# One tile and one cadence for the modulation sums of a hybrid mLSTM and gated-delta block, from the first solve pairs to the last output product

## The chip, the cores and the metric

The kernel runs on one core of a Trainium2 chip. A core has a matrix engine (TensorE, "PE" in the profile, with its weight loads as "PEld"), a vector engine (VectorE, "DVE"), a scalar engine (ScalarE, "ACT"), GpSimd ("POOL"), and a queue engine SyncE ("SP") that issues most of the loads. Sixteen DMA engines carry the transfers of all queues. Each engine works through its own stream of instructions in order; semaphores order the streams among each other.

The metric is the device time in microseconds (us) of one execution. The program was run three times before the change, and the median counts.

## What is computed

One layer of a bidirectional block on 256 tokens of 2048 channels. Cut to what matters here:

```python
mod = c_act @ ada_w + ada_b          # c_act = silu(c): one row of 2048; ada_w: 2048 x 12288
shift_m, scale_m, gate_m, shift_f, scale_f, gate_f = jnp.split(mod[:, None, :], 6, axis=-1)
h = rms_norm(x, norm_mix_w) * (1 + scale_m) + shift_m
proj = h @ w_in                       # q, k, v, gates of both branches, merge gates
y_a = (sigmoid(a_o) * rms(mlstm_bidir(...))) @ w_branch_a
y_b = (rms(gated_delta_bidir(...)) * silu(b_z)) @ w_branch_b
x = x + gate_m * ((g_a * y_a + g_b * y_b) @ w_out)
hf = rms_norm(x, norm_ffn_w) * (1 + scale_f) + shift_f
gt, up = jnp.split(hf @ w_gate_up, 2, axis=-1)
x = x + gate_f * ((silu(gt) * up) @ w_down)
out = rms_norm(x, norm_final_w)
```

The gated delta branch has 16 heads; each needs the inverse of unit lower triangular 64 x 64 matrices, made here by block inversion.

## The kernel before

**Products.** Every weight matrix is used once. A job loads it in pieces of 1 MB through SP into the tile `raw` (three buffers). ACT rounds each half of a piece to the high part `wh`, DVE subtracts to get the low part `wl` (three buffers each), and TensorE multiplies high by high, high by low and low by high. `fjob` makes 128 output channels from one piece; `tjob` makes 512 output channels from four pieces (weights 512 wide, 12 products to a half). After the products of each half stands a call of `pump()`. So the whole kernel has a count of halves, and that count is used in this document: half n is the one whose products stand just before the n-th call of `pump()`. It was counted by going through the loops by hand.

**The modulation sums.** Parts 0 and 1 of `mod` are made in the first stage. Parts 2 (`gate_m`), 3 (`shift_f`) and 4 (`scale_f`) are made later, 16 columns of 128 values each, so 48 sums. One sum is a load of 1 MB (tile `ada`, issued on SP by `ask()`, L116) and one DVE instruction that multiplies 128 x 2048 values with the broadcast row and adds them up (`add()`, L124). Part 5 (`gate_f`, 16 sums) follows in the FFN with a cadence of eight halves. Where `ask` and `add` go is decided in `pump()` and `sums()`:

- `every[0]`: a sum is owed at each call whose count is a multiple of it; 0 means none is owed and none is asked for.
- `held[0]`: true in the first three of the nine steps of a solve pair; while it is true nothing is added.
- `age[0]`: calls of `pump()` since the last `ask()`. A sum is added only if that is over two.
- `room[0]`: the pool, the tag, the number of buffers and the number of transfers that may be outstanding. At first it is one tile (`rows_p`, tag `ada`). From the a-branch's output product on it is a pool `sr` with three tiles, and then `sums()` keeps three transfers asked for ahead of each sum.

Instructions wrapped in `order(...)` are kept behind the instruction that stands before them on their engine; others may be moved ahead of them by the scheduler, which lays out each engine's stream when the program is built. `ask` and `add` are wrapped; the loads and splits of a `tjob` are not.

**The stages around the change.**

1. Four groups g = 0 to 3 of four heads. Before each group a triangular inversion (`gdn_invert`): DVE makes 32 x 32 inverses, POOL stores them (L696) and loads them back in another layout into `cg` (L723), DVE transposes `cg` (L725) and mixes it to `R` (L729, L730), ACT copies parts to `X` (L738). The first solve product (L761, `p<-R,cc`) needs `R`. Meanwhile TensorE works on product jobs (`fill`).
2. In each group two pairs of heads go through `gdn_phase2` (nine steps), between them the `fjob`s of the next heads (`b_job`) and their `gdn_phase1`. In groups 0 to 2 the pairs span halves 63 to 94, 118 to 149 and 173 to 204; in group 3 halves 228 to 253.
3. The first two mLSTM heads and the rest of the merge gates, to half 258; the b-branch's output product `y_b` (halves 259 to 290) beside the mLSTM heads; the a-branch's output product `y_a` (291 to 322); there `gate_m` is spread over the partitions (`row_diag`, `row_spread`, at halves 292, 296, 300, 304) and the merged branches are transposed (`merged`).
4. The last output product `o_job` 0 to 3 (halves 323 to 350 and the last piece of job 3, which goes by tokens). Before its end all of parts 3 and 4 must be there: `sums(P)` makes what is left, and `affn` is made of part 4. Then RMSNorm, and the FFN.

**Where the sums stand before the change**, by this count: the adds of group 0 at halves 67, 71, 75, 84, 88, 92, those of groups 1 and 2 at the same distances from their start (122, 126, 130, 139, 143, 147 and 177, 181, 185, 194, 198, 202), those of group 3 at 232, 236, 240, 245, 249, 253. Each `ask` follows one half after the add before it; the seventh, 13th and 19th are asked for at halves 93, 148 and 203, at the end of a group, and wait through the inversion. After the pairs there are none until half 270; then adds at 273, 277, 281, 285 and 289, one more at the end of `y_b`, three transfers asked for at once at the start of `y_a`, adds at 291, 292 and every fourth half to 320, and nine in the output product at 327, 330, 333, 336, 341, 344, 347, 349 and 351.

Of the kernel before, what the change touches and what calls it, by code (L numbers as in the profile page):

```python
# [9 lines left out]
F32 = mybir.dt.float32  # L10
# [5 lines left out]
P = 128  # L16
T = 256
D = 2048
# [34 lines left out]
def hybrid_block(ctx: ExitStack, tc: tile.TileContext, xr, nfr, crow, pk_d, cst_d, ada2, ada4, win0, winb, wint, wba, wbb, wo, wgu, wd, out, dbg=None):  # L53
# [3 lines left out]
    def pool(stack, name, bufs=1, **kw):  # L57
        return stack.enter_context(tc.tile_pool(name=name, bufs=bufs, **kw))
# [3 lines left out]
    rows_p = pool(ctx, "rows")  # L62
# [9 lines left out]
    def order(ins, yes=True):  # L72

        return tc.keep_in_program_order(ins) if yes else ins
# [30 lines left out]
        order(S.activation(row_c[:, g * 512 : (g + 1) * 512], pc_, AF.Silu))  # L105


    room = [(rows_p, "ada", 1, 1)]
    asked, unasked, age = [], [], [0]

    def ask():

        pl, tag, bufs, _ = room[0]
        part, b = unasked.pop(0)
        raw = pl.tile([P, D], F32, tag=tag, bufs=bufs, name=f"ada{part}_{b}")
        order(nc.sync.dma_start(raw, ada4[part - 2, b]))  # L116
        asked.append((part, b, raw))
        age[0] = 0

    def add():  # L120

        part, b, raw = asked.pop(0)
        c = part * KB + b
        order(V.scalar_tensor_tensor(raw, raw, 1.0, row_c[:, :D], ALU.mult, ALU.mult, accum_out=mod[:, c : c + 1]))  # L124
        if b == KB - 1:
            c = slice(part * KB, part * KB + KB)
            V.tensor_tensor(mod[:, c], mod[:, c], pk[:, PK_ADAB + c.start : PK_ADAB + c.stop], ALU.add)
# [11 lines left out]
    def settle(keep=0, only=None):  # L139

        now = [f for f in behind if only is None or f.__name__ == only]
        for f in now[: len(now) - keep]:
            behind.remove(f)
            f()

    count, every = [0], [0]
    owed, held = [0], [False]

    def sums(n=1):

        while n and (unasked or asked):
            while unasked and len(asked) < room[0][3]:
                ask()
            add()
            n -= 1

    def pump():
        count[0] += 1
        age[0] += 1
        if every[0] and count[0] % every[0] == 0:  # L160
            owed[0] = 1
        if room[0][3] > 1:
            if owed[0]:
                owed[0] = 0
                sums()
        elif asked:
            if owed[0] and age[0] > 2 and not held[0]:
                owed[0] = 0
                add()
        elif unasked and every[0]:  # L170
            ask()

    def fjob(name, src, done):
# [95 lines left out]
    def fill(n=1):  # L269

        while n and fills:
            if next(fills[0], None):
                n -= 1
            else:
                fills.pop(0)
# [90 lines left out]
    def z_job(g, early=0):  # L366
        def done(ps):
            szs[g] = evp.tile([P, 2, 512], F32, tag="sz", bufs=1, name=f"sz{g}")
            for t in range(2):
                S.activation(szs[g][:, t], ps[t], AF.Silu)  # L370
        return tjob(f"z{g}", [wint[g, u] for u in range(4)], hh, hl, done, early)
# [121 lines left out]
    with ExitStack() as s0:  # L493
# [18 lines left out]
        def loads(b):  # L512
            ra = [w0.tile([P, D + 2], F32, tag="ra", bufs=5, name=f"ra{b}_{i}") for i in range(2)]
            raw = st.tile([P, N0, P], F32, tag="raw", bufs=3, name=f"raw0_{b}")
            for i in range(2):
                order(nc.sync.dma_start(ra[i], ada2[b, :, i]))
            order(nc.sync.dma_start(raw, win0[b]))
            return ra, raw
# [10 lines left out]
        ra, raw = loads(0)  # L529
# [18 lines left out]
        for b in range(KB):  # L548
            if b:
                ra, raw = loads(b)  # L550
# [137 lines left out]
    def gdn_invert(g):  # L688

        uu = uus.pop(g)  # L690
        tmp = bk.tile([64, 256], F32, tag="utmp", bufs=1, name=f"utmp{g}")
        inv = inv_d[g].rearrange("j b (x h) i -> h (b x) j i", h=GRP)

        def store(rows):
            for e in range(GRP):
                G.dma_start(inv[e, :, rows], uu[16 * e : 16 * e + 16, rows])  # L696

        yield
        order(V.memset(uu.rearrange("p j i -> p (j i)")[:, ::33], 1.0))
        size = 0  # L700
        for i in range(30, 0, -1):
            w = 31 - i
            t3 = tmp[:, 0 : i * w].rearrange("p (j c) -> p j c", j=i)
            order(V.tensor_tensor(
                t3,
                uu[:, 0:i, i : i + 1].broadcast_to([64, i, w]),
                uu[:, i : i + 1, i + 1 :].broadcast_to([64, i, w]),
                ALU.mult,
            ))
            order(V.tensor_tensor(uu[:, 0:i, i + 1 :], uu[:, 0:i, i + 1 :], t3, ALU.add))  # L710
            if i == 16:
                store(slice(16, 32))
            size += i * w + 125
            if size > 720:
                size = 0
                yield
        store(slice(0, 16))
# [300 lines left out]
    def invert(g):  # L1018
        gen = gdn_invert(g)
        next(gen)  # L1020
        fill(4 if g else 6)
        for _ in gen:
            fill(1)

    invert(0)
    for g in range(4):
        blocks = gdn_blocks(g)
        next(blocks)
        fill(8)
        next(blocks)  # L1030
        fill(1)
        pairs = [gdn_phase2(g, p) for p in range(2)]
        if g == 3:
            settle()
            sf.close()
            mq["pool"] = pool(sq_, "mq", side="right")
            first2 = [mlstm(h) for h in range(2)]
            for c in first2:
                next(c)
        every[0] = 1  # L1040
        for p in range(2):
            pieces = stream(4 * g + 2 * p + 4)
            for n in range(1, 10):

                held[0] = n < 4
                if p == 0:
                    next(blocks, None)
                next(pairs[p], None)
                if g == 3 and n == (8, 4)[p]:
                    next(first2[p])  # L1050
                for _ in range(last[n] if g == 3 else second[n] if p else after[n]):
                    next(pieces)
            for _ in pairs[p]:
                pass

            if g < 3:
                while 4 * g + 2 * p + 5 not in heads:
                    next(pieces)
        if g < 3:
            fills.insert(0, z_job(g + 1))  # L1060
            every[0] = owed[0] = 0
            invert(g + 1)
    settle()
    sx.close()
# [53 lines left out]
            yield from y_b(g)  # L1118

    o4s = [o_load(g) for g in range(2)]  # L1120
    every[0] = owed[0] = 0
    cores = steps(*first2)
    fill(1)
    next(cores)
# [19 lines left out]
    o_split(3, o4s[3])  # L1144
    fill(2)
    drive(cores, 3)
    every[0] = 1
    drive(steps(mlstm(2), mlstm(3)), 3)
    fill(1000)
    mgh, mgl = big(bigC, F32R, "mgh"), big(bigC, F32R, "mgl")  # L1150
    sm_.close()
    sr_ = ExitStack()
    if asked:
        add()
    room[0] = (pool(sr_, "sr"), "sr", 3, 3)
    gm = room[0][0].tile([P, D], F32, name="gm")
    dgs = {}

    def row_diag(part, g, rp):
        ms = mods[:, part == 5]  # L1160
        if not g:
            m = mod[:, part * KB : (part + 1) * KB]
            V.tensor_copy(ms[:, 0], m)
            V.tensor_tensor(ms[:, 1], m, ms[:, 0].bitcast(F32), ALU.subtract)
        dg = dgs[part, g] = rp.tile([P, 2, 4, P], F32R, tag="dg", bufs=2, name=f"dg{part}_{g}")
        for i in range(2):
            V.tensor_tensor(
                dg[:, i], ident.unsqueeze(1).broadcast_to([P, 4, P]),
                ms[:, i, 4 * g : 4 * g + 4].bitcast(F32).unsqueeze(2).broadcast_to([P, 4, P]), ALU.mult,
            )  # L1170
# [6 lines left out]
            PE.matmul(pr, onesr, woven(dg[:, i]), start=i == 0, stop=i == 1)  # L1177
        S.activation(woven(dst[:, g * 512 : (g + 1) * 512]), pr.rearrange("p (c h) -> p c h", h=2), AF.Copy)

    every[0] = 4  # L1180
    for g in range(4):
        for i, _ in enumerate(y_a(g)):
            if g and i == 3:
                merged(g - 1, mgh, mgl)
            if i in (1, 5) and g < 2:
                row_diag(2, 2 * g + i // 4, room[0][0])
            if i in (3, 7) and g < 2:
                row_spread(2, 2 * g + i // 4, gm)
    every[0] = 0


    def o_job(g, front=None):
# [112 lines left out]
    for g in range(4):  # L1305
        if g == 3:
            root()
        for i, _ in enumerate(o_job(g, front_o if g == 3 else None) if g else o_first, 0 if g else 2):
            if i in ((4, 7), (2, 5), (2, 5), (0, 2))[g]:
                sums()  # L1310
            if g == 3 and i == 4:
                sums(P)
                V.scalar_tensor_tensor(
                    affn, mod[:, 4 * KB : 5 * KB], 1.0, pk[:, PK_NFFN : PK_NFFN + KB], ALU.add, ALU.mult
                )
    if dbg is not None and "x1" in dbg:
        G.dma_start(dbg["x1"], x1)
    room[0] = (rows_p, "ada", 1, 1)
    ada_parts(5)
    sw.close()  # L1320
    sr_.close()
# [73 lines left out]
    for j in range(FB // 4):  # L1395
# [4 lines left out]
        for e2 in range(2):  # L1400
            px = gps(f"pxf{j}_{e2}")
            for e in range(2):
                f = 2 * e2 + e
                for t in range(2):
                    PE.transpose(px[:, e * T + t * P : e * T + (t + 1) * P], sg[:, t, f * P : (f + 1) * P], ident)
            b = 4 * j + 2 * e2
# [156 lines left out]
```

## Time and profile before

| | us |
|---|---|
| median of three runs | 1973.17 |
| lowest and highest of the three | 1971.56 and 1974.83 |
| the profiled execution, its own time | 1974.3 |
| its span in the trace | 1972.4 |

The profile page gives, by engine, the busy time and its share of the span. The view of windows gives the same for chosen stretches, with the granted clock of TensorE (1.00 is full speed) and the share in which the DMA engines were busy. The view of waits says for which instruction another engine stood idle, in total, how often, and the longest. The timeline gives start and duration in us of each instruction of one engine, with the idle time before it and what ended it in brackets. `SPq`, `POOL DMA` rows are issues: the transfer itself ends later. A row "DMA to landing" gives the time from issue to the last byte.

### The profile page before, as it was taken

The numbers are of one execution on the slowest core, as the hardware profiler recorded it, in microseconds if no ns is written. First come the engines' busy times: TensorE is split into PE (matmuls) and PEld (weight loads), VectorE is DVE, ScalarE is ACT, GpSimd is POOL, SyncE is SP. The second block draws the span as 40 slices with busy tenths as digits, with TensorE's granted clock in tenths as the row PEclk, the third lists the DMA queues.
The fourth block names the chain that finished last, engine by engine and source line by source line (L and its number), as shares of the span: only waits on it lengthen the run. The fifth ranks groups of instructions, "written<-read, shape, count | busy, mean of one in ns | idle before, by whom it ended". The sixth has DMA issues, their size and how long they took to land.

```text
span 1972.4 us, 27079 instructions
## 1 busy us (share of the span) xinstructions
PE 1929.4 (98%) x10418; PEld 1703.5 (86%) x10418; DVE 1405.5 (71%) x2067; ACT 1030.0 (52%) x1555; POOL 116.5 (6%) x211
## 2 busy tenths in 40 slices
PE   8999999999999999999999999999999999999998
PEld 6878889998998899889787888888888888888886
DVE  6779887887888798866577878866665665555554
ACT  3137656764766577565544444644444444444444
POOL 0001210111001010110100000200000000000000
PEclk9999999999999999999999999999999999999999
DMA  9987676766566666586777888566676665565663
GB/s 399 420 349 226 184 249 240 252 214 208 203 217 213 237 218 229 192 296 246 277 282 266 323 317 330 191 252 238 238 265 241 237 238 205 197 213 197 208 199 142
DMA packets 78962, 485.64 MB, mean 246 GB/s; under 512 B 10585, under 2 KB 15969, under 8 KB 24433
## 3 DMA queue, kind: packets, MB, share of 16 engines
q1 hardware_dynamic: 63216, 450.69, 62.9%
q0 software_dynamic: 8160, 17.88, 4.5%
q10 hardware_dynamic: 7458, 15.36, 2.1%
q8 instruction: 81, 1.33, 0.3%
q14 instruction: 47, 0.39, 0.1%
HBM read 467.07 MB, written 16.82 MB: 245 GB/s over the span
## 4 chain that ended last, share of the span: by engine, by line
PE 81%; DVE 8%; DMA 6%; ACT 2%; issue 1%; POOL 0%; ACTq 0%; SPq 0%; DVEq 0%; POOLq 0%
PE acc_gt L234 4%; PE acc_gt L235 4%; PE acc_gt L236 4%; PE acc_up L236 4%; PE acc_up L235 4%; PE acc_up L234 4%; PE acc_d L236 4%; PE acc_d L235 4%; PE acc_d L234 4%; DMA ra<-ada 3%; PE acc_b L187 2%; PE acc_b L188 2%; PE acc_b L189 2%; PE acc_o L236 2%; PE acc_o L234 2%; PE acc_o L235 2%
## 5 line engine op out<-in xcount | busy, mean ns | idle before, releaser
L215 DVE TENSOR_TENSOR wl_d<-raw_d,wh_d 128x1024 fp32r<-128x1024 f32 x88 | 107.7, 1224 | 105.9 <-ACT wh_d L213 105.9
L215 DVE TENSOR_TENSOR wl_up<-raw_up,wh_up 128x1024 fp32r<-128x1024 f32 x88 | 107.7, 1224 | 100.2 <-ACT wh_up L213 100.1
L215 DVE TENSOR_TENSOR wl_gt<-raw_gt,wh_gt 128x1024 fp32r<-128x1024 f32 x88 | 108.1, 1229 | 80.2 <-ACT wh_gt L213 80.2
L187 PE MATMUL acc_b<-hh,wh_b 128*128 128x256 f32 x576 | 163.0, 283 | 0.6 <-ACT wh_b L182 0.6
L189 PE MATMUL acc_b<-hh,wl_b 128*128 128x256 f32 x576 | 159.6, 277 | 0.8 <-DVE wl_b L184 0.8
L188 PE MATMUL acc_b<-hl,wh_b 128*128 128x256 f32 x576 | 159.2, 276 | 0.0
L213 ACT ACTIVATE wh_d<-raw_d 128x1024 fp32r<-128x1024 f32 x88 | 92.9, 1056 | 126.5 <-PE acc_d L235 117.7
L213 ACT ACTIVATE wh_gt<-raw_gt 128x1024 fp32r<-128x1024 f32 x88 | 92.9, 1056 | 118.6 <-PE acc_gt L235 71.1
L213 ACT ACTIVATE wh_up<-raw_up 128x1024 fp32r<-128x1024 f32 x88 | 92.8, 1055 | 108.1 <-PE acc_up L235 77.1
L124 DVE SCALAR_TENSOR_TENSOR ada<-ada,crow 128x2048 f32<-128x2048 f32 x64 | 146.0, 2284 | 0.0
L234 PE MATMUL acc_gt<-wh_gt,hfh 128*128 128x512 f32 x352 | 135.6, 385 | 0.6 <-ACT hfh L1350 0.6
L235 PE MATMUL acc_gt<-wh_gt,hfl 128*128 128x512 f32 x352 | 134.9, 383 | 0.0
L236 PE MATMUL acc_gt<-wl_gt,hfh 128*128 128x512 f32 x352 | 134.1, 381 | 0.0
L234 PE MATMUL acc_up<-wh_up,hfh 128*128 128x512 f32 x352 | 133.4, 379 | 0.0
L235 PE MATMUL acc_up<-wh_up,hfl 128*128 128x512 f32 x352 | 133.4, 379 | 0.0
L236 PE MATMUL acc_up<-wl_up,hfh 128*128 128x512 f32 x352 | 133.4, 379 | 0.0
L234 PE MATMUL acc_d<-wh_d,ffh 128*128 128x512 f32 x344 | 130.5, 379 | 0.0
L235 PE MATMUL acc_d<-wh_d,ffl 128*128 128x512 f32 x344 | 130.5, 379 | 0.0
L236 PE MATMUL acc_d<-wl_d,ffh 128*128 128x512 f32 x344 | 130.4, 379 | 0.0
L561 PE MATMUL first<-x,raw 128*128 128x256 f32 x512 | 114.5, 382 | 7.2 <-ACT x L555 7.2
L561 PEld LDWEIGHTS first<-x,raw 128*128 128x128 f32 x512 | 96.0, 190 | 25.7 <-ACT x L555 13.3
L189 PEld LDWEIGHTS acc_b<-hh,wl_b 128*128 128x128 f32 x576 | 111.3, 193 | 1.0 <-DVE wl_b L184 1.0
(383 smaller groups left out, 5263.1 us busy)
## 6 DMA issues: line engine op xcount, KB each, us to landing
ada<-ada SPq DMA_DIRECT2D x64, 1024.0 KB, 6.0
raw_gt<-wgu SPq DMA_DIRECT2D x44, 1024.0 KB, 4.9
raw_up<-wgu SPq DMA_DIRECT2D x44, 1024.0 KB, 4.9
raw_d<-wd SPq DMA_DIRECT2D x44, 1024.0 KB, 4.9
raw_b<-winb SPq DMA_DIRECT2D x36, 1024.0 KB, 5.3
ra<-ada SPq DMA_DIRECT2D x32, 1025.0 KB, 15.8
raw<-win SPq DMA_DIRECT2D x16, 1024.0 KB, 14.5
raw_z<-wint SPq DMA_DIRECT2D x16, 1024.0 KB, 5.0
```

Of the source, the lines that this page charges most:

```text
L124: order(V.scalar_tensor_tensor(raw, raw, 1.0, row_c[:, :D], ALU.mult, ALU.mult, accum_out=mod[:, c : c + 1]))
L187: PE.matmul(o, wh[:, k], woven(hh[:, kk]), start=kk == 0, stop=False)
L188: PE.matmul(o, wh[:, k], woven(hl[:, kk]), start=False, stop=False)
L189: PE.matmul(o, wl[:, k], woven(hh[:, kk]), start=False, stop=kk == KB - 1)
L213: order(S.activation(wh, raws[u][:, k0 : k0 + 2], AF.Copy), early)
L215: order(V.tensor_tensor(wl, raws[u][:, k0 : k0 + 2], wh.bitcast(F32), ALU.subtract), early)
L234: order(PE.matmul(ps[t], xh[:, kk, c], woven(wh[:, k]), start=kk == 0, stop=False), early and steps > 1)
L235: PE.matmul(ps[t], xl[:, kk, c], woven(wh[:, k]), start=False, stop=False)
L236: PE.matmul(ps[t], xh[:, kk, c], woven(wl[:, k]), start=False, stop=kk == last)
L561: PE.matmul(first[o], raw[:, o], x[:, b], start=b == 0 and o % 2 == 0, stop=b == KB - 1 and o % 2 == 1)
```

## The change

- The second pool of tiles for the sums is gone: the one tile of `rows_p` serves to the end. `sums()` asks only if nothing is outstanding.
- One cadence: `every[0]` stays 1 from the first pair of group 3 through the mLSTM heads, `y_b`, `y_a` and the output product up to its job 3, half 350. The four explicit calls of `sums()` per output job and the cadence of 4 in `y_a` are gone. After the pairs of group 3 `held` is cleared, and the sums go on.
- A pause `calm`: `age` now also restarts at an add, and the next `ask` comes `calm[0]` halves after the add, two in groups 0 to 2, one elsewhere.
- `sums(P)` and `affn` move from half 351 to half 350.

By the same count the adds after the change stand at 67, 72, 77, 84, 89, 94 in group 0 and at the same distances in groups 1 (122 to 149) and 2 (177 to 204), unchanged in group 3, and then at every fourth half from 257 to 349: 18 + 6 + 24 = 48, so nothing is left for `sums(P)`. The asks that open groups 1, 2 and 3 stand at halves 118, 173 and 228, the first of their pairs, as that of group 0 always did at half 63. In the FFN nothing moves.

```diff
-    room = [(rows_p, "ada", 1, 1)]
     asked, unasked, age = [], [], [0]
     def ask():
-        pl, tag, bufs, _ = room[0]
         part, b = unasked.pop(0)
-        raw = pl.tile([P, D], F32, tag=tag, bufs=bufs, name=f"ada{part}_{b}")
+        raw = rows_p.tile([P, D], F32, tag="ada", name=f"ada{part}_{b}")
...
-    owed, held = [0], [False]
+    owed, held, calm = [0], [False], [1]
     def sums(n=1):
         while n and (unasked or asked):
-            while unasked and len(asked) < room[0][3]:
+            if not asked:
                 ask()
             add()
             n -= 1
...
         if every[0] and count[0] % every[0] == 0:
             owed[0] = 1
-        if room[0][3] > 1:
-            if owed[0]:
-                owed[0] = 0
-                sums()
-        elif asked:
+        if asked:
             if owed[0] and age[0] > 2 and not held[0]:
-                owed[0] = 0
+                owed[0] = age[0] = 0
                 add()
-        elif unasked and every[0]:
+        elif unasked and every[0] and age[0] >= calm[0]:
             ask()
...
         every[0] = 1
+        calm[0] = 2 if g < 3 else 1
...
             every[0] = owed[0] = 0
+            calm[0] = 1
             invert(g + 1)
...
-    every[0] = owed[0] = 0
+    held[0] = False
     cores = steps(*first2)
...
-    every[0] = 1
     drive(steps(mlstm(2), mlstm(3)), 3)
...
-    if asked:
-        add()
-    room[0] = (pool(sr_, "sr"), "sr", 3, 3)
-    gm = room[0][0].tile([P, D], F32, name="gm")
+    sr = pool(sr_, "sr")
+    gm = sr.tile([P, D], F32, name="gm")
...
-    every[0] = 4
     for g in range(4):
         for i, _ in enumerate(y_a(g)):
...
-    every[0] = 0
...
-            if i in ((4, 7), (2, 5), (2, 5), (0, 2))[g]:
-                sums()
-            if g == 3 and i == 4:
+            if g == 3 and i == 3:
+                every[0] = owed[0] = 0
                 sums(P)
...
-    room[0] = (rows_p, "ada", 1, 1)
     ada_parts(5)
```

More of the change, by code (lines that the diff above doesn't have):

```diff
@@ L1185, in hybrid_block @@
             if i in (1, 5) and g < 2:
-                row_diag(2, 2 * g + i // 4, room[0][0])
+                row_diag(2, 2 * g + i // 4, sr)
             if i in (3, 7) and g < 2:
                 row_spread(2, 2 * g + i // 4, gm)
-    every[0] = 0
     def o_job(g, front=None):
```

## The prediction

> **What bounds the kernel now.** I read the page first, then the stages, then who waits for whom.
>
> ```profile
> span 1972.4 us, 27079 instructions
> PE 1929.4 (98%) x10418; PEld 1703.5 (86%) x10418; DVE 1405.5 (71%) x2067; ACT 1030.0 (52%) x1555; POOL 116.5 (6%) x211
> ```
>
> TensorE is busy for 98% of the span. Whatever this change wins or loses must show as idle time, or as slow time, of TensorE. By stage (busy columns: PE, PEld, DVE, ACT, POOL, then clock, DMA share, GB/s):
>
> ```profile
> core 0: us, PE busy (x) PEld busy (x) DVE busy (x) ACT busy (x) POOL busy (x), PEclk, DMA share, GB/s
> 940.00:983.00 43.00, 43.00 (x191) 33.54 (x190) 26.03 (x41) 25.35 (x38) 9.33 (x15) 1.00 0.75 265
> 1069.00:1103.00 34.00, 30.15 (x134) 25.08 (x133) 30.23 (x39) 14.64 (x20) 0.00 (x0) 0.95 0.98 376
> 1103.00:1171.00 68.00, 68.00 (x328) 59.52 (x327) 54.12 (x57) 30.97 (x33) 0.00 (x0) 1.00 0.81 302
> ```
>
> TensorE has no idle time where the b-branch's product begins (940 to 983), nor in the rest of `y_a` (1103 to 1171), where a sum already stands at every fourth half. It has 3.85 us idle in 34 at the start of `y_a`, where DVE is busy for 30 of 34 us and the DMA engines are full. What ended TensorE's waits from 300 to 1260 us (total, times, longest):
>
> ```profile
> PE acc_ya L236 <- DVE wl_ya L215: 3.8, 2, 2.2
> PE vps L609 <- ACT vf L341: 2.7, 3, 1.4
> PE acc_z L234 <- ACT wh_z L213: 2.5, 1, 2.5
> PE acc_o L236 <- DVE wl_o L215: 1.1, 2, 0.8
> ```
>
> The longest line is the entry of `y_a`. On DVE, and then on TensorE:
>
> ```profile
> 1078.58 2.28 DVE L124 SCALAR_TENSOR_TENSOR ada<-ada,crow 128x2048 f32<-128x2048 f32 x1
> ...
> 1083.01 2.28 DVE L124 SCALAR_TENSOR_TENSOR ada<-ada,crow 128x2048 f32<-128x2048 f32 x1
> ...
> 1085.22 1.22 DVE L215 TENSOR_TENSOR wl_ya<-raw_ya,wh_ya 128x1024 fp32r<-128x1024 f32 x1
> ```
>
> ```profile
> 1080.29 0.38 PE L234 MATMUL acc_ya<-wh_ya,hah 128*128 128x512 f32 x1
> ...
> 1082.88 0.38 PE L234 MATMUL acc_ya<-wh_ya,hah 128*128 128x512 f32 x1
> ...
> 1086.49 0.93 PE L236 MATMUL acc_ya<-wl_ya,hah 128*128 128x512 f32 x2 [2.15 <-DVE wl_ya L215]
> ```
>
> A half of twelve products takes 1082.88 - 1080.29 = 2.59 us. The next one needs its low part, and that stands behind three sums in a row (1078.58 to 1085.22). Two more things follow:
>
> ```profile
> 1069.74 3.39 SPq L116 DMA_DIRECT2D ada<-ada  x4
> 1083.12 2.54 SPq L116 DMA_DIRECT2D ada<-ada  x2
> 1100.90 0.48 PE L236 MATMUL acc_ya<-wl_ya,hah 128*128 128x512 f32 x1 [1.66 <-DVE wl_ya L215]
> ```
>
> ```profile
> 1087.00:1090.00 3.00, 3.00 (x8) 2.34 (x8) 3.00 (x4) 0.79 (x2) 0.00 (x0) 0.50 0.98 295
> 790.00:798.00 8.00, 5.45 (x20) 3.86 (x19) 5.96 (x14) 5.89 (x13) 2.68 (x5) 0.79 0.20 57
> ```
>
> Six sums' transfers within 16 us fill the DMA engines, weights come late, and TensorE waits again, for 1.66 us. And after the first wait TensorE runs at half clock: eight products in 3.00 us, where twelve take 2.59.
>
> **The change part by part.**
>
> *The burst at the entry of `y_a` goes.* By the count of halves no sum stands between halves 289 and 293, where three stood. That takes 3 x 2.28 = 6.8 us of DVE work from ahead of the late low part, more than the 2.15 us it was late, and spreads the six transfers. Both waits go: **-3.8**. The half clock goes with them. The 0.79 over 790 to 798 is a dip too, 8 x 0.21 / 0.5 = 3.4 us at half speed, and the wait of 2.5 us for `wh_z` lies there. A dip costs half its length, and I take the one at 1087 to be as long: **-1.7**. The Trainium skill ("TensorE: Matmul & The Clock Gate", Part 1) lets the clock fall only after about 3.4 us of idle window; by that the 2.15 us wait would not have caused the dip and the sum below would be 1.7 us smaller. This trace shows a clock of 0.50 right behind a 2.15 us wait, and the measurement decides.
>
> *The output product.* Nine sums become seven, evenly spaced. Of the 1.1 us of the `acc_o` waits, 0.8 lies in an inversion, 0.3 here: **-0.3**. Nothing is left for `sums(P)`, and `affn` has its last sum four halves, 10 us, before the job's end.
>
> *The asks that open groups 1 to 3* move. Before, they waited through the inversion with the data long landed. Now each is the first thing behind the first load of its pair on SP, where group 0's is. POOL's small gather `cg` flies just then. Its four loads by group, and DVE's wait for them:
>
> ```profile
> 298.16 0.43 SPq L116 DMA_DIRECT2D ada<-ada  x1
> ...
> 299.99 1.99 POOL L723 DMA_DIRECT2D cg<-inv_d  x4 [5.08 <-DMA inv_d<-uu]
> ...
> 482.32 1.99 POOL L723 DMA_DIRECT2D cg<-inv_d  x4 [5.00 <-DMA inv_d<-uu]
> ...
> 665.26 1.99 POOL L723 DMA_DIRECT2D cg<-inv_d  x4 [5.52 <-DMA inv_d<-uu]
> ...
> 841.18 2.00 POOL L723 DMA_DIRECT2D cg<-inv_d  x4 [5.85 <-DMA inv_d<-uu]
> ```
>
> ```profile
> 309.56 0.71 DVE L725 STREAM_TRANSPOSE cg<-cg 128x512 f32<-128x512 f32 x1 [3.74 <-DMA cg<-inv_d]
> ...
> 489.73 0.71 DVE L725 STREAM_TRANSPOSE cg<-cg 128x512 f32<-128x512 f32 x1 [3.62 <-DMA cg<-inv_d]
> ...
> 670.55 0.71 DVE L725 STREAM_TRANSPOSE cg<-cg 128x512 f32<-128x512 f32 x1 [1.08 <-DMA cg<-inv_d]
> ...
> 673.33 0.48 DVE L730 SCALAR_TENSOR_TENSOR R<-cg,cst,R 128x256 f32<-128x256 f32 x1
> ...
> 848.04 0.71 DVE L725 STREAM_TRANSPOSE cg<-cg 128x512 f32<-128x512 f32 x1 [0.18 <-DMA cg<-inv_d]
> ```
>
> First load to transpose takes 9.57 us in group 0, where the sum's transfer flies beside it; 7.41, 5.29 and 6.86 in the others. At the upper end they all become 9.57: +2.2, +4.3, +2.7. Behind the transpose stand `R`, the copies to `X` and the next splits, in order. In group 1 TensorE already waits there, so its 2.2 counts in full:
>
> ```profile
> 493.33 0.38 PE L187 MATMUL acc_b<-hh,wh_b 128*128 128x256 f32 x1 [0.56 <-ACT wh_b L182]
> 674.94 0.97 PE L761 MATMUL p<-R,cc 128*128 128x32 f32 x8
> ```
>
> In group 2 `R` is ready at 673.8 and used at 674.9, so 1.1 of 4.3 is hidden; I take group 3 as hidden by the product jobs, as TensorE shows no wait there. Upper end 2.2 + 3.2 = 5.4, and with a clock dip at both places 8.8. The lower end is 0: before, each gather also flew beside loads of 1 MB, and one more behind them in SP's queue need not delay POOL's queue. I take **+1.5**, below the middle. The load that the ask of group 1 will follow is this one on SP:
>
> ```profile
> 478.31 5.51 SPq L178 DMA_DIRECT2D raw_b<-winb  x2
> ```
>
> The gather there starts 4.0 us behind it, in group 0 only 1.8 us behind the ask itself, so less of the added transfer is ahead of it.
>
> *New sums from half 257 to 269*, where none stood. The tight place is the second sum, behind the first low part of 975.72:
>
> ```profile
> 975.72 1.23 DVE L215 TENSOR_TENSOR wl_yb<-raw_yb,wh_yb 128x1024 fp32r<-128x1024 f32 x1 [0.73 <-ACT wh_yb L213]
> 976.86 1.22 DVE L1081 TENSOR_TENSOR obl<-o,obh 128x1024 fp32r<-128x1024 f32 x1
> 977.99 2.35 DVE L215 TENSOR_TENSOR wl_yb<-raw_yb,wh_yb 128x1024 fp32r<-128x1024 f32 x2
> ```
>
> ```profile
> 980.79 0.38 PE L236 MATMUL acc_yb<-wl_yb,obh 128*128 128x512 f32 x1
> ```
>
> The next low part would end at 979.2 + 2.3 = 981.5 and is first used at 980.79: 0.7 late. Three more transfers come into 40 us at a DMA share of 0.75; weights there have cover of two pieces. I take **+0.7**, between 0 (the scheduler puts the low part ahead of `obl`) and one whole sum and a dip, 2.3 + 1.7 = 4.0.
>
> *Inside the pairs* twelve of 18 sums move back by one or two halves. The waits that sums may touch are `vps` and `acc_z`. Ends: the `acc_z` wait and its dip vanish, -4.2, because the sum ahead of that chain moves behind it; or a sum falls on another such chain, +4.0. I take **-0.5**, as the first is a place that I can name.
>
> Sum: -3.8 - 1.7 - 0.3 + 1.5 + 0.7 - 0.5 = **-4.1**. The profiled execution took 1974.3 (its span 1972.4 and 1.9 around it); it becomes 1970.2. The median of the runs shown is 1.1 below that execution: **1969.1**.
>
> **The rivals.**
>
> *The gather is hit in full.* +8.8 in place of +1.5: 1976.4. For it: group 0 is the same code with the same ask. Against it: the gathers of groups 1 to 3 differ by 2.1 us among each other with no sum beside them, so the 9.57 may not be the sum's doing.
>
> *The one tile's round trip is longer than the cadence* in `y_a` and the output product, and the kernel is slower than before. With one tile, an ask can go only when the add before it is done. Four halves are 10.36 us.
>
> ```profile
> L124 DVE SCALAR_TENSOR_TENSOR ada<-ada,crow x15: 2283/2284/2286, 1108.5 to 1243.0; 128x2048 f32<-128x2048 f32 x15
> ```
>
> ```profile
> DMA to landing us min/median/max: 4.8/5.8/8.2
> ```
>
> Those are the sums and transfers of 1105 to 1245. Sum and landing take 2.28 + 5.8 = 8.1 at the median and 10.5 at the most. If the ask also stands on SP behind a weight load that waits a half for its buffer, 2.59 more: 10.7 to 13.1. It decides from a landing of 5.5 us on. DVE then waits in order with the low parts behind it. If every third of the 14 sums is 2.7 late, 12.6: 1981.7. Against it: between 1010 and 1070 us one tile served as well, and no wait of TensorE is listed there. The Trainium skill ("Trainium Kernel Development and Optimization", Best Practices) advises two buffers, so that transfers overlap with work; by that rule this rival is what to expect, but the trace's one-tile stretches do not bear it out.
>
> *The wait in `y_a` stays in part*, since splits of the mLSTM result and `row_diag` still crowd DVE at the entry; half of 5.8 is won: 1972.0.
>
> *The wait for `wh_z` goes with its dip*: 3.7 more than I took: 1965.4.
>
> *The change does not do what it says*: one sum is left for `sums(P)`, and DVE waits for its transfer and makes it, 8.1, at the end of the output product: 1977.2.
>
> **How the numbers follow.** Forecast 0.40 (its own range 1967 to 1971.2), gather 0.16, round trip 0.12, wait in part 0.13, `wh_z` 0.15, one left over 0.04. About 0.2%, 3.9 us, is what a measurement of this kernel can tell from no change: below 1969.2 is faster, above 1977.1 slower. The forecast stands on the edge: half of it, and all of `wh_z`, is faster: 0.20 + 0.15 = 0.35. Slower: the round trip, half of the left-over, and 0.06 of the gather: 0.20. The rest, 0.45, is the same. The range leaves out the round trip and some 0.05 at the low end: 1964.5 to 1978.5.
>
> **What would show it.** No wait of over 0.5 us in `acc_ya`, and a clock of 1.00 from 1070 to 1110; a sum at every fourth half there, with no three in a row. First gather load to transpose under 9 us in groups 1 to 3, and no TensorE wait behind it that was not there. No DVE wait on `ada`. I am wrong if DVE waits for `ada` in `y_a` or the output product, if `cg` takes over 9 us, or if the clock dips at 1086 without a wait.

## The result, and the profile after

The changed kernel takes 1978.88 us in the median of eleven runs (1976.22 to 1982.44), the kernel before 1973.17 in eleven runs beside it. The ratio is 1.0026, with a 95% interval of 1.0017 to 1.0034: **slower by 5.1 us** (3.4 to 6.7), where 4.1 us of gain were forecast. The two medians differ by 5.7 us; the forecast's range ended at 1978.5. The profiled execution took 1976.22 us, 1.9 more than the one of before. It is the fastest of its eleven. Three executions of over 3200 us, one each of e4, of e6 and of the kernel before beside e6, were in a slow state and are left out of all medians and ratios.

What ended TensorE's waits from 300 to 1260 us (total, times, longest), in the changed kernel:

```profile
PE vps L603 <- ACT vf L335: 6.8, 8, 1.4
PE acc_z L228 <- ACT wh_z L207: 3.0, 1, 3.0
...
PE acc_o L230 <- DVE wl_o L209: 0.8, 1, 0.8
...
```

`acc_ya` is gone from the list, as forecast. But `vps` went from 2.7 us in 3 waits to 6.8 in 8. Smaller new waits follow further down, instruction by instruction. (The line numbers are 6 lower than before in most of the file; `vps` was L609.) By stretch of time, first before and then after, with the columns of the prediction's table:

```profile
310.00:459.00 149.00, 146.73 (x1054) 138.05 (x1053) 130.16 (x260) 106.52 (x207) 16.21 (x32) 1.00 0.67 217
495.00:642.00 147.00, 143.50 (x1082) 137.00 (x1081) 125.85 (x252) 101.41 (x199) 16.14 (x32) 0.99 0.66 213
680.00:841.00 161.00, 156.91 (x1164) 148.61 (x1163) 137.94 (x282) 110.36 (x208) 16.78 (x32) 0.99 0.65 218
```

```profile
310.00:459.00 149.00, 145.24 (x1045) 136.35 (x1044) 128.01 (x256) 106.15 (x207) 16.23 (x32) 1.00 0.64 209
495.00:642.00 147.00, 141.54 (x1079) 134.67 (x1079) 125.64 (x251) 103.04 (x204) 15.69 (x32) 1.00 0.63 205
680.00:841.00 161.00, 154.38 (x1154) 146.17 (x1153) 135.89 (x278) 111.49 (x209) 14.55 (x28) 0.98 0.60 206
945.00:1075.00 130.00, 128.72 (x576) 103.89 (x575) 93.67 (x130) 63.64 (x96) 9.87 (x16) 0.99 0.78 287
1069.00:1103.00 34.00, 33.96 (x165) 29.47 (x164) 30.78 (x38) 17.18 (x22) 0.00 (x0) 1.00 0.84 297
```

The first three are the pairs of groups 0 to 2. TensorE's idle time there (the length less the first busy column) goes from 2.27 + 3.50 + 4.09 = 9.9 us to 3.76 + 5.46 + 6.62 = 15.8: 6.0 lost. The entry of `y_a` (1069 to 1103) goes from 3.85 to 0.04 at a clock of 1.00.

**One of the new waits, instruction by instruction.** In the changed kernel, 355 to 366 us (start, duration, engine, line, operation, tiles; in brackets the wait ahead of it):

```profile
359.39 0.47 DVE L332 SCALAR_TENSOR_TENSOR cv<-pad,pk,cv 128x256 f32<-128x256 f32 x1
359.79 2.28 DVE L122 SCALAR_TENSOR_TENSOR ada<-ada,crow 128x2048 f32<-128x2048 f32 x1
...
362.00 0.48 DVE L332 SCALAR_TENSOR_TENSOR cv<-pad,pk,cv 128x256 f32<-128x256 f32 x1
...
362.91 1.22 DVE L209 TENSOR_TENSOR wl_ma<-raw_ma,wh_ma 128x1024 fp32r<-128x1024 f32 x1
364.05 0.48 DVE L332 SCALAR_TENSOR_TENSOR cv<-pad,pk,cv 128x256 f32<-128x256 f32 x1
364.56 0.42 ACT L335 ACTIVATE vf<-cv 128x256 f32<-128x256 f32 x1 [2.84 <-DVE cv L332]
365.03 0.44 PE L603 MATMUL vps<-cst,vf 128*128 128x128 f32 x2 [1.17 <-ACT vf L335]
```

`cv` is the last convolution of a head: four taps on DVE, each on the result of the one ahead. `vf` is its Silu on ACT, `vps` its transposition on TensorE. The third sum of the pair stands between the first tap and the second, and the whole chain stands still for 2.28 us. (A split of 1.22 us, `wl_ma`, stands between the third tap and the fourth as well; e4 below has such a split in the chain without the sum, and no wait.) Before, the same sum ran ahead of the chain:

```profile
355.08 2.28 DVE L124 SCALAR_TENSOR_TENSOR ada<-ada,crow 128x2048 f32<-128x2048 f32 x1
...
358.42 0.48 DVE L338 SCALAR_TENSOR_TENSOR cv<-pad,pk,cv 128x256 f32<-128x256 f32 x1
...
361.68 0.42 ACT L341 ACTIVATE vf<-cv 128x256 f32<-128x256 f32 x1 [1.48 <-DVE cv L338]
```

`vf` begins 2.9 us earlier there, and no wait follows. This is not one place but six: the third sum of both pairs, in each of three groups. In the second pair it stands between the second tap and the third (the sums of 420.48, 604.21 and 785.31). In the changed kernel the other waits are:

```profile
424.19 0.44 PE L603 MATMUL vps<-cst,vf 128*128 128x128 f32 x2 [0.71 <-ACT vf L335]
...
547.07 0.44 PE L603 MATMUL vps<-cst,vf 128*128 128x128 f32 x2 [0.41 <-ACT vf L335]
...
607.92 0.44 PE L603 MATMUL vps<-cst,vf 128*128 128x128 f32 x2 [0.62 <-ACT vf L335]
...
729.14 0.44 PE L603 MATMUL vps<-cst,vf 128*128 128x128 f32 x2 [1.19 <-ACT vf L335]
...
798.18 0.80 PE L228 MATMUL acc_z<-wh_z,hh 128*128 128x512 f32 x1 [2.95 <-ACT wh_z L207]
...
800.93 1.22 PE L230 MATMUL acc_z<-wl_z,hh 128*128 128x512 f32 x2 [0.68 <-DVE wl_z L209]
```

The first pair's place recurs every 182 us (365, 547, 729), the second pair's every 184 (424, 608); its third time comes out as the `wh_z` wait, 2.95 + 0.68 where 2.5 stood before. Together 1.17 + 0.71 + 0.41 + 0.62 + 1.19 + 1.1 = **5.2 us**. Half of the last term may not be the sum's: in e2, e6, e8 and e10 below, with that sum in its old place, `wl_z` waits 0.56 behind a `wh_z` wait of 2.51, and against those the total is 4.7.

At this last place the loss takes another way, over ACT. Before, and then in the changed kernel:

```profile
780.12 0.42 ACT L341 ACTIVATE vf<-cv 128x256 f32<-128x256 f32 x1 [1.82 <-DVE cv L338]
```

```profile
787.54 1.28 ACT L335 ACT_TABLE_LOAD   x1
788.83 0.42 ACT L335 ACTIVATE vf<-cv 128x256 f32<-128x256 f32 x1
```

`vf` comes after ACT has turned to other functions, and a load of a function table stands ahead of it. Between the chain and `wh_z` there are five such loads of 1.28 us on ACT in the changed kernel, in e3 and in e4, and four before and in all runs that leave this sum ahead of the chain. That fits a longer `wh_z` wait, but no run takes the load away by itself.

**Late by how much, where.** For each kernel the table gives its lag behind the profiled execution of before at some places: the median of the differences of ACT's start times, over the instructions within 8 us of the place that occur equally often in both kernels. The names are those of the experiments below; e1 to e10 stand for the kernels whose labels begin so.

```
before's us:  300   440   520   680   785   850   945  1000  1075  1110  1300
after        -0.3  +1.3  +2.0  +3.4  +4.5  +7.4  +7.0 +10.2  +8.5  +2.0  +1.8
e1           +0.3  +0.1  -0.2  -1.8  -1.7  -0.4  -0.4  +3.4  +1.7  -4.8  -5.0
e2           -0.6   0.0  +1.3  +1.5  +1.2  +0.9  +0.9  +4.7  +4.7  -1.3  -2.2
e3            0.0  +2.6  +4.0  +5.4  +6.5 +10.0  +9.5 +10.1 +10.1 +10.1  +8.5
e4           -0.9  +1.8  +2.9  +3.0  +5.9  +8.0  +7.8 +11.2  +9.6  +3.1  +2.6
e5           -0.1  +0.1  +2.1  +4.8  +4.9  +5.2  +5.0  +8.6  +8.6  +2.1  +1.9
e6           -0.1  -0.2  -0.2   0.0   0.0  +1.4  +1.4  +4.6  +4.6  -1.8  -2.0
e8           -1.1  -2.1  -1.7  -3.3  -3.2  -2.7  -2.7  -0.3  -2.0  -8.4  -8.7
e9           +0.3  -0.7  -0.3  -0.2  -0.2  +0.2   0.0  +0.1  +0.1  -5.4  -5.1
e10          -0.5  -1.2  -1.1  -2.2  -2.2  -2.1  -2.1  +0.9  +0.9  -5.4  -5.8
```

The changed kernel is 7.4 us late when the pairs of group 2 and the inversion behind them are done, loses a little more up to 1075, and wins 6.5 at the entry of `y_a`. Steps of 1.7 within a row are periods at half clock that one execution has and the other has not. The row of e5 is mostly that: its profiled execution, 1976.42 us, is the slowest of its twelve, and between 490 and 805 us it has five such steps where before has two, 3 x 1.7 = 5.1.

### The profile page after: what moved, and what is told of

Read it like the earlier page. It is cut to its first block, busy times and chain, and to the rows that moved or that the text cites. A ratio compares the mean times of both kernels' runs of the same rounds, so it can differ in the third digit from the quotient of the medians.

```text
span 1974.2 us, 27081 instructions
## 1 busy us (share of the span) xinstructions
PE 1927.8 (98%) x10418; PEld 1701.0 (86%) x10418; DVE 1405.3 (71%) x2067; ACT 1031.4 (52%) x1556; POOL 116.5 (6%) x211
## 6 DMA issues: line engine op xcount, KB each, us to landing
ra<-ada SPq DMA_DIRECT2D x32, 1025.0 KB, 15.8
```

## The experiments

**Theory A:** sums that the change moves inside the pairs cost what is lost there, because they now stand inside a chain of short DVE operations. **Rival B:** the asks that open groups 1 to 3 fly beside the small gather and cost it. **Rival C:** the pairs are a symptom, and the longer stretch of single sums from half 257 on costs it. All runs are five rounds beside the kernel before; ratios are to it, and 0.001 is 2.0 us. They ran on three chips (e1 to e4; e5, e8 and e9; e6 and e10), so differences between experiments are taken from the ratios.

**e1: the pairs as before, the rest as changed.**

```
         every[0] = 1
-        calm[0] = 2 if g < 3 else 1
         for p in range(2):
...
             every[0] = owed[0] = 0
-            calm[0] = 1
             invert(g + 1)
```

> The changed kernel without the pause in the pairs: the sums and asks of all four groups' pairs stand where they stood before the change, the asks that open groups 1 to 3 go out ahead of the inversion again; everything behind the pairs is as changed. Theory A (the moved sums in the pairs cost the 7.4 us that the changed kernel is late at 850 us, the entry of y_a gives 6.6 back): no vps wait of over 0.5 us but the two of before (1.4 and 1.0), y_a still without a wait, time 1978.9 - 7.4 = 1971.5, ratio to before 0.999. Rival B (the opening asks beside the small gather cost it): also 1971.5, told apart by e2. Rival C (the pairs are a symptom and the loss comes from the longer stretch of single sums from half 257 on): stays above 1976.

Measured: 1971.68 us, ratio 0.9988 (0.9977 to 0.9998). The `vps` waits are back at three:

```profile
PE vps L603 <- ACT vf L335: 2.8, 3, 1.5
```

Rival C falls: the loss comes from what the change does to the pairs, their opening asks included, and what is left of the change is a small gain.

**e2: as e1, but with the opening asks where the change has them.** Here and in e4 to e6 the pairs of groups 0 to 2 follow a table: halves of the group at which an ask, and at which a sum, is issued.

```
     def pump():
         count[0] += 1
         age[0] += 1
+        if plan[0]:
+            k = count[0] - plan[0][0]
+            if k in plan[0][1]:
+                ask()
+            if k in plan[0][2]:
+                add()
+            return
...
-        calm[0] = 2 if g < 3 else 1
+        plan[0] = (count[0], (1, 6, 10, 14, 23, 27), (5, 9, 13, 22, 26, 30)) if g < 3 else None
```

> As e1, but the asks that open groups 1 to 3 stay where the change puts them, in the first half of the pair; the 18 sums of the pairs stand where they stood before the change. Theory A: as e1, within 1.5 us (the gather's part by the trace: 0.4 us in group 1, 1.1 us in group 2), 1971.5 to 1973. Rival B (the asks beside the gather): the whole loss is here, 1977 or more, and the gather takes 8 to 9 us from first load to transpose in groups 1 and 2.

Measured: 1973.78 us, ratio 0.9996 (0.9982 to 1.0010): 1.6 us above e1, with an uncertainty of 3.5 from the two intervals. Rival B in its full form, 1977 or more, falls. Something of it is real, as its sign for the gather holds: from first load to transpose it takes 8.0 us in group 1 and 8.4 in group 2 here, 7.3 and 5.6 in e1. DVE's waits for the gather (total, times, longest), in e1 and then in e2:

```profile
DVE cg L719 <- DMA cg<-inv_d: 8.2, 3, 3.6
```

```profile
DVE cg L728 <- DMA cg<-inv_d: 12.8, 3, 4.4
```

**e3: the pair part alone, in the kernel before.**

```
         every[0] = 1
+        calm[0] = 2 if g < 3 else 1
         for p in range(2):
...
-                owed[0] = 0
+                owed[0] = age[0] = 0
                 add()
-        elif unasked and every[0]:
+        elif unasked and every[0] and age[0] >= calm[0]:
```

> The kernel before with the pair part of the change alone: the pause of two halves before an ask in groups 0 to 2, the rest of the kernel with its burst at the entry of y_a. Theory A: before + 7.4 = 1980.6, and up to 1984 if the medians differ as those of the two kernels do; the y_a wait of 3.8 us is still there. Rival C: within 1.5 us of before.

Measured: 1982.89 us, ratio 1.0049 (1.0034 to 1.0063), 9.7 us slower. Its waits show both things side by side, the eight of `vps` and the untouched entry of `y_a`:

```profile
PE vps L609 <- ACT vf L341: 6.8, 8, 1.4
PE acc_ya L236 <- DVE wl_ya L215: 3.8, 2, 2.2
```

So the pair part costs 7 to 12 us by itself, and with e1's gain of 2.4 taken off it gives +7.3, against +5.1 (3.4 to 6.7) for the whole change; the intervals cover that.

**e4: only the third sum of each pair moved.** As e2, with six of the 18 sums two halves later:

```
-        plan[0] = (count[0], (1, 6, 10, 14, 23, 27), (5, 9, 13, 22, 26, 30)) if g < 3 else None
+        plan[0] = (count[0], (1, 6, 12, 17, 23, 29), (5, 9, 15, 22, 26, 32)) if g < 3 else None
```

> As e2, but with the third sum of each pair of groups 0 to 2 (six sums) two halves later, where the change has it: between the first and the second tap of the last convolution's chain on DVE, ahead of vf and of vps. The other twelve sums stand as before the change. Theory A in its narrow form (it is the sum inside that chain, not the moving as such): most of the 7.4 us is back, e2 + 5 to 7, and vps waits of 0.4 to 1.2 us stand in both pairs. If it is the number of sums moved, or the later asks, e2 + 3 at most, and the vps waits are the two of before.

Measured: 1981.26 us in eight runs, ratio 1.0037 (1.0023 to 1.0050), 8.1 us above e2, with an uncertainty of 3.8. These six sums bring the loss back, and the waits with it:

```profile
PE vps L612 <- ACT vf L344: 6.4, 7, 1.4
```

There are seven `vps` waits and not eight, and the missing one is a test of its own. In the second pair of group 1 the scheduler put the fourth tap ahead of the sum here:

```profile
605.05 0.48 DVE L341 SCALAR_TENSOR_TENSOR cv<-pad,pk,cv 128x256 f32<-128x256 f32 x1
605.45 2.29 DVE L122 SCALAR_TENSOR_TENSOR ada<-ada,crow 128x2048 f32<-128x2048 f32 x1
```

`vps` follows at 606.92 without a wait, although a split of 1.22 us stands between the third tap and the fourth. The same sum, at the same half, cost 0.62 in the changed kernel, where two taps stood behind it. So five of the six sums stand inside the chain in e4.

**e5: the third sum of the first pair behind the chain.** The sharpest test of "inside the chain" against "later": as e1, with this sum still one half later than the change has it.

```
+        plan[0] = (count[0], (1, 6, 13, 17, 23, 27, 31), (5, 9, 16, 22, 26, 30)) if g < 3 else None
...
-            if k in plan[0][1]:
+            if k in plan[0][1] and not asked:
```

> As e1, but the third sum of the first pair of groups 0 to 2 stands three halves later than before the change, one half later than the change has it, and so behind the last convolution's chain on DVE instead of inside it. All other sums stand as in e1. If the place inside the chain costs, and not the moving back: as e1 within 1.5 us (1970 to 1973.5), and no vps wait at about 365, 547 and 729 us. If a later sum as such costs, at least what the chain showed in the first pairs, 1.17 + 0.41 + 1.17 = 2.75: 1974.5 or more, with the waits in place.

Measured: 1970.82 us, ratio 0.9981 (0.9971 to 0.9991), as e1. The taps run together, and the sum follows them:

```profile
360.27 1.52 DVE L341 SCALAR_TENSOR_TENSOR cv<-pad,pk,cv 128x256 f32<-128x256 f32 x3
361.83 0.48 DVE L341 SCALAR_TENSOR_TENSOR cv<-pad,pk,cv 128x256 f32<-128x256 f32 x1
...
362.35 0.42 ACT L344 ACTIVATE vf<-cv 128x256 f32<-128x256 f32 x1 [2.03 <-DVE cv L341]
...
366.99 2.28 DVE L122 SCALAR_TENSOR_TENSOR ada<-ada,crow 128x2048 f32<-128x2048 f32 x1
```

None of the three `vps` waits of the first pairs is there. Moving the sum further back takes its cost away, although the chain begins later here (360.27) than in the changed kernel (359.39). For the second pair this was not tried, as three halves later is already in the inversion; there the one case in e4 stands for it.

**e6: second and third sum of the first pair one half later.**

```
+        plan[0] = (count[0], (1, 6, 11, 15, 23, 27, 31), (5, 10, 14, 22, 26, 30)) if g < 3 else None
```

> As e1, but in the first pair of groups 0 to 2 the second and the third sum stand one half later than before the change (the change has the second one half and the third two halves later); there the third is still ahead of the last convolution's chain. The second pair's sums stand as in e1. If only a sum inside the chain costs: as e1 within 1.5 us, ratio to before 0.998 to 0.9995, no vps wait at about 365, 547 and 729 us. If the second sums or moving as such cost: 1974.5 or more.

Measured: 1971.43 us in eleven runs, ratio 0.9981 (0.9968 to 0.9994), as e1, with the three `vps` waits of before. At one half later the third sum is still ahead of the chain (356.38, where the taps begin at 358.59). In the first pair neither moving as such nor the second sum costs anything that can be seen.

**e8: no sums in the entry of `y_b`, and a closer cadence behind it.** This asks for the smaller loss between 945 and 1075 us.

```
+    every[0] = owed[0] = 0
     held[0] = False
     cores = steps(*first2)
...
     drive(cores, 3)
+    every[0] = 1
...
+    room[0], every[0] = (sr, "sr", 2), 3
...
+        if room[0][2] > 1:
+            if owed[0] and asked:
+                owed[0] = 0
+                add()
+            elif unasked and every[0] and len(asked) < 2:
+                ask()
```

> As e1, but with no sum from half 254 to 269 (the entry of the b-branch's product), as before the change; the four sums that this takes away are made up by a cadence of three halves, from two tiles, in y_a and the output product. Theory: the new sums in the entry of the b-branch's product cost what e1's profile is late between 945 and 1000 us, 3.8 us (of which 1.7 can be a clock dip that falls there by chance): the profile is then within 0.5 us of before's there, and the time is e1 - 2 to e1 - 3.8, 1968 to 1969.7, if the closer cadence costs nothing. If it does, acc_ya or acc_o waits of over 0.5 us stand from 1080 us on. Rival: the loss at 945 to 1000 us is the clock alone and stays: 1971.7.

Measured: 1966.17 us, ratio 0.9956 (0.9940 to 0.9971): the fastest kernel here, faster than the kernel before and the changed one, and below the range that was expected. But the reason that was given for it holds only in part: by the table its profile still loses 2.4 us to that of before between 945 and 1000, where at most 0.5 was expected. From 945 to 1075 us, before and then e8:

```profile
945.00:1075.00 130.00, 129.96 (x587) 104.80 (x586) 88.36 (x121) 64.11 (x94) 9.86 (x16) 0.99 0.76 276
```

```profile
945.00:1075.00 130.00, 128.09 (x581) 102.87 (x580) 89.02 (x121) 63.42 (x93) 9.89 (x16) 1.00 0.76 277
```

Idle time is 0.04 us before, 1.3 in the changed kernel and 1.9 in e8, which has one other wait there:

```profile
PE ph L980 <- ACT hs L982: 1.8, 1, 1.8
```

In the six other kernels with sums in that entry it is 0.95 (e10) to 3.05 us (e2), 2.1 in the mean with the changed kernel; in e3 and e9, without them, 0.3 and 0.04. So the sums do cost there, though in e8's profile another wait takes their place. It has two steps at half clock from 300 to 1300 us, e10's profile four.

**e9: the burst at the entry of `y_a` alone spread, in the kernel before.**

```
-    if asked:
-        add()
     room[0] = (pool(sr_, "sr"), "sr", 3, 3)
...
-            if i in ((4, 7), (2, 5), (2, 5), (0, 2))[g]:
+            if i in ((2, 4, 7), (1, 3, 5), (2, 5), (0, 2))[g]:
```

> The kernel before with its burst at the entry of y_a alone spread: the sum that is asked for when the b-branch's product ends is the first of the cadence of four, and two sums more stand in the output product. Pairs, y_b and the tiles are before's. If the y_a step of the prediction was right: no acc_ya wait, before - 3.8 and up to - 5.5 with the clock: 1968 to 1970. If the three transfers that are asked for at once make the weights late by themselves: the second wait of 1.7 us stays, 1971 to 1972.5.

Measured: 1968.61 us, ratio 0.9967 (0.9954 to 0.9979), 6.5 us faster, and 5.5 of it between 1075 and 1110 us in the table. What is left of the entry's waits, and what the two more sums brought to the output product:

```profile
PE acc_o L236 <- DVE wl_o L215: 2.3, 2, 1.5
...
PE acc_ya L236 <- DVE wl_ya L215: 0.3, 1, 0.3
```

**e10: e8's cadence without its quiet entry.**

```
-    every[0] = owed[0] = 0
     held[0] = False
     cores = steps(*first2)
...
-    every[0] = 1
```

> As e8 with its cadence of three halves from two tiles from the first half of y_a on, but with the sums from half 254 to 269 as in e1 and in the changed kernel; the sums so come to their end some halves earlier in the output product. If e8's gain over e1 is the quiet entry of the b-branch's product: as e1, ratio to before 0.998 to 1.000, and the profile late by 2 to 4 us between 945 and 1000 us. If it is the cadence and the two tiles: as e8, ratio 0.9945 to 0.997.

Measured: 1970.94 us, ratio 0.9976 (0.9965 to 0.9986), between e1 and e8. The difference to e8 is 3.9 us with an uncertainty of 3.7. That the quiet entry is worth something is likely, but how much of e8's lead is its doing, and how much the clock's, stays open.

## Why the prediction was wrong

**The step that failed is "Inside the pairs": -0.5, taken between -4.2 and +4.0.** The runs show 5.2 us of named waits in its place (rows above), 8.1 us with an uncertainty of 3.8 by e4 against e2, and 6.7 to 12.4 by e3 together with the opening asks. The prediction knew the danger ("or a sum falls on another such chain, +4.0") but priced it once. Twelve sums move, but there are only four different moves, since three groups run the same program; a bad place is met three times. Two of the four moves, the third sum of either pair by two halves, put the sum between two taps; the runs find no cost of the others. And the value was taken from "the first is a place that I can name": the `wh_z` wait was to vanish because the sum ahead of its chain moves behind it. That sum (774.65 before) is the third one of the second pair in group 2. It moved not behind the chain but into it (785.31), and the wait grew. Nor does a row of the kernel before tie that wait to the sum: `vf` starts at 780.12, `vps` follows at 782.53 without a wait, and `wh_z` stands later in ACT's own queue, where it starts at 792.30 behind `obt`. So the gain of up to 4.2 had no wait for the sum under it; whether a sum behind the chain would change it, no run shows.

The other steps, by their own numbers:

- **Burst at `y_a`, -3.8, and the half clock, -1.7:** right. No `acc_ya` wait is left, the clock is 1.00, the lag falls by 6.5 there; in e9, where nothing else changes up to that place, by 5.5. In e3 the wait of 2.15 us stands, and the half clock behind it too (1097.12).
- **Output product, -0.3:** right. Of `acc_o` only the wait of 0.8 in an inversion is left.
- **Opening asks, +1.5:** right in size. The gather's rows in groups 1 and 2, and what TensorE then waits for:

```profile
483.52 1.99 POOL L717 DMA_DIRECT2D cg<-inv_d  x4 [4.82 <-DMA inv_d<-uu]
...
491.51 0.71 DVE L719 STREAM_TRANSPOSE cg<-cg 128x512 f32<-128x512 f32 x1 [4.03 <-DMA cg<-inv_d]
...
666.72 1.99 POOL L717 DMA_DIRECT2D cg<-inv_d  x4 [5.51 <-DMA inv_d<-uu]
...
675.44 0.71 DVE L719 STREAM_TRANSPOSE cg<-cg 128x512 f32<-128x512 f32 x1 [4.51 <-DMA cg<-inv_d]
```

```profile
495.11 0.38 PE L181 MATMUL acc_b<-hh,wh_b 128*128 128x256 f32 x1 [0.97 <-ACT wh_b L176]
...
676.96 1.08 PE L755 MATMUL p<-R,cc 128*128 128x32 f32 x8 [0.40 <-DVE R L724]
...
691.64 1.10 PE L789 MATMUL p<-X,pt 128*128 128x64 f32 x8 [0.69 <-DVE pt L778]
```

  First load to transpose takes 7.99 and 8.72 us (7.41 and 5.29 before). TensorE pays 0.97 - 0.56, 0.40 and 0.69: 1.5. The sign "no TensorE wait behind it that was not there" failed all the same. The rival "hit in full" gave 1976.4, not far from the result, but by a cause that is worth 1.5.
- **New sums in the entry of `y_b`, +0.7 (0 to 4.0):** right in kind, too small: 1.3 in the changed kernel, 2.1 in the mean of seven. In time it may be more: e9 is 4.1 us below e1, with an uncertainty of 3.2, though the two differ in the output product too. Part of it came from the round trip, which the prediction looked for only from `y_a` on. In the changed kernel:

```profile
997.00 2.29 DVE L122 SCALAR_TENSOR_TENSOR ada<-ada,crow 128x2048 f32<-128x2048 f32 x1 [1.38 <-DMA ada<-ada]
...
1000.49 0.48 PE L230 MATMUL acc_yb<-wl_yb,obh 128*128 128x512 f32 x1 [0.54 <-DVE wl_yb L209]
...
1006.26 0.44 PE L988 MATMUL pxa<-cst,hs 128*128 128x128 f32 x2 [0.75 <-DVE hal L993]
```

  The sum waits 1.38 us for its transfer, the low part stands behind it on DVE, and TensorE waits. It is the only wait of DVE for a sum's transfer in the changed kernel; in `y_a` and the output product, where that rival stood, there is none.

With the two terms as measured the sum closes: -4.1 + 0.5 + 5.2 + 0.6 = +2.2, against 1.9 between the two profiled executions. That it closes so well is partly luck. Its -1.7 stands for one half-clock step less, and up to 1300 us the profile does have four such steps where before had five; but those at 582, 1025 and 1087 are gone, and a second one at 798 and one at 959 are new, and only the one at 1087 was planned.

The median moved by more, 5.1 to 5.7: the profiled execution after is the fastest of its kind, and the one before stood 1.1 above its median. The other ten executions of the changed kernel lie 2.8 us above the profiled one in the mean. Their granted clocks say most of why: 0.9938 in the mean where the profiled one had 0.995, and 0.0012 of 1976 us is 2.4 us. This is an estimate from clocks that are listed in thousandths, and single executions scatter around it.

The list of signs had none for the pairs. Sums that move there were the largest number of edits, and the list watched only the places where a gain or a known risk stood.

## What to carry to other kernels

A piece of work that is pinned into an in-order queue cost here by what stands behind it, not by its own length or its distance: 2.28 us between two taps of a chain cost 0.4 to 1.2 us each time, ahead of the chain or behind it nothing that could be seen. Before such pieces are moved, list for each new place the instruction ahead and behind, and multiply by the passes of the loop around it, since one bad place in a loop's body can be paid in every pass. Look at each pass all the same: in e4 the scheduler laid one of the passes out differently, and that one cost nothing. And separate the parts: here the wanted half of the change alone (e9, -6.5 us) and the half that came with it (e3, +9.7 us) had opposite signs.

## What the runs showed of the hardware

The half-clock periods of TensorE keep to a grid. In the trace's clock records of before they begin at 581.65, 793.28, 1025.38, 1086.82 and 1260.90 us, which are 62, 68, 18 and 51 steps of 3.413 us apart; each lasts one such step, and two in the changed kernel at 798.12. The grid lies differently against the program in each execution, so the same wait may or may not be followed by a period: the 2.5 us wait for `wh_z` brings one of two steps in e1, one of one step in e6, and none in e2. Each step costs about 1.7 us. The Trainium skill ("TensorE: Matmul & The Clock Gate", Part 1) gives a window of about 3.4 us, and this grid agrees with that. It lets the clock fall after an idle window; here 1.0 to 3.0 us of idle time within a step were at times enough (the `vps` wait of 1.17 us that ends at 728.69 in e4 is followed by one at 730.39), and some periods begin with no idle time ahead of them, as this one in e1, with the stretch before it:

```profile
945.00:951.60 6.60, 6.60 (x46) 6.12 (x45) 3.19 (x5) 3.02 (x6) 0.00 (x0) 1.00 0.82 297
951.70:955.10 3.40, 3.40 (x9) 2.70 (x8) 0.45 (x4) 0.07 (x1) 2.59 (x4) 0.50 0.98 406
```

What sets these off no run here shows. Where the border of the steps falls counts too. In e2 the 2.5 us wait for `wh_z` lies across one, 1.8 us in one step and 1.3 with the waits after it in the next, and no half clock followed. In the eleven traces, from 300 to 1310 us, each of the 15 steps with over 2.0 us of idle time was followed by half clock; of those with 1.0 to 1.9 us some were and some were not. For a forecast it means that a term for the clock, such as the -1.7 of this one, is a chance and not a sum.
